# Two more pairs of gate blocks by quarter sums, and the pooling's output product moved into the attention

## The chip, the cores and the metric

The kernel runs on one core of a Trainium2 chip. The metric is the device time of one execution in microseconds (us). Before the change three runs took 1218.12, 1218.23 and 1218.29 us; the median is 1218.23.

## The reference

One layer of a streaming encoder on 1024 tokens (and 16 meta tokens ahead of them) of width 1024, all in float32:

```python
z = jnp.einsum('bld,dn->bln', u, w_in)             # u: RMS-normed input
a, q, k, v, r, lr, ga, gb = jnp.split(z, IN_SPLITS, axis=-1)   # 512, 256, 256, 512, 512, 16, 1024, 1024
p = multiscale_pool(a).reshape(B, L, POOL_GROUPS, POOL_GROUP_DIM)
p = jnp.einsum('blgc,gce->blge', p, w_pool_mix).reshape(B, L, POOL_WIDTH) * pool_scale
y_a = jnp.einsum('blc,cd->bld', p, w_pool_out)
log_a = jax.nn.log_sigmoid((lr @ w_gate_up + b_gate)) / GLA_TAU
...
o = gla_chunked(q, k, v, log_a)                    # gated linear attention, chunks of 64
o = rmsnorm(o, gla_norm) * jax.nn.silu(r)
y_b = jnp.einsum('blc,cd->bld', o, w_gla_out)
m = jax.nn.sigmoid(ga) * y_a + jax.nn.sigmoid(gb) * y_b
return jnp.einsum('bld,de->ble', m, w_out)         # then h + this, and a squared-ReLU MLP 1024-4096-1024
```

## The kernel before

**Products.** A float32 product is made of three passes (`mm3`, L250 to 257): high part by high part (L255), weights' high part by the input's low part (L256), weights' low part by high part (L257). So each operand is first split: the high part is a copy (ScalarE), the low part a subtraction (VectorE, or GpSimd in the attention). The input is kept split in `TH` and `TL`, one tile for each half of the 1024 tokens (`th`, `tl` in rows). A block is 128 columns of an output; over 1024 tokens it is 8 pieces of depth by two halves by three passes, 48 matmuls of 512 columns. Weights of a block come from HBM to a raw buffer and are split into `W1` (`w1h`, `w1l`; L83 and L87, in the attention four quarters on GpSimd).

**Stages, in the order in which TensorE runs them.** (1) Load, norm and split of the input, first values. (2) *Gate stage*: the class `Quarters` takes two blocks and both halves of the depth as a product of 2 by 2 parts, and makes it with 7 products of quarter sums in place of 8, so a pair of blocks is 7 x 12 = 84 matmuls in place of 96. `BLOCKS` lists the 16 blocks, 8 pairs: the eight of gate `ga`, two of the queries `q`, four of `r`, two of gate `gb`. Results go to HBM (`ga_dram`, `q_dram`, `r_dram`, `gb_dram`). (3) *Pooling*: four groups (`a_block`, `mean_block`, `mix_block`): the product `a`, the trailing means minus the token (`ph`, high and low), and six matmuls of the mixing. An eviction on ScalarE (L918) and one on VectorE (L919) write the pooled operand `pm` as high and low part. (4) *Pool output product*: `ya_block`, four blocks of 256 columns and 48 matmuls each, of depth 512; a unit of it (12 matmuls) is evicted by VectorE with a multiplication by the gate (L971) into `o` and stored to `ma_dram`. Group 0 is mixed inside the first block. The gates are loaded by `gate_load` into six buffers `g`. (5) *Attention*, `gla`: four units, each one pair of heads by one half of the tokens, and between their steps *filler*, so that TensorE has work while VectorE and ScalarE make scores and states: key blocks, the values' second half, six blocks of `gb` (direct, 48 matmuls each, with a sigmoid of several ScalarE and VectorE steps, L926 to 930, and an exponential), and the output product `yb`. (6) Output projection and the two MLP products, also by quarter sums.

**What sets the order.** Within a stage each engine runs its instructions in the order in which the program records them. `one` lists the steps, `fill` the filler's; `pour` takes filler by an estimate of its cost for each wait of the attention's steps. DMAs are issued by SyncE, a single queue in order; an issue that waits for a buffer holds up all behind it. Two stacks of on-chip memory, `left` and `right`, are pushed and popped at the stages' borders, so tiles of a later stage lie in the room of earlier ones, and their first writers wait for the last readers.

**Names that the steps below use.** `lr`: the 16 rows of the low-rank gate, stacked three times (`stacked`, L538 to 546: a clearing on GpSimd, two copies on ScalarE, a subtraction on VectorE), multiplied at L1170 (L1183 in the changed program) for the log-decay of a unit. `scc`: scores after the masked copy (L1290), from products at L1227. `f`, `n`: the decayed operands on VectorE (L1259, L1261). `b_...`: PSUM banks by role.

Of the kernel before, what the change touches and what calls it, by code (L numbers as in the profile page):

```python
# [15 lines left out]
P = 128  # L16
# [98 lines left out]
def kernel(  # L115
# [84 lines left out]
    def f32(ap):  # L200
        return ap.bitcast(F32)
# [49 lines left out]
    def mm3(ps, n, lhs, rhs, first=True, last=True, more=False):  # L251

        for i in range(n):
            (ah, al), (bh, bl) = lhs(i), rhs(i)
            pe.matmul(ps, ah, bh, start=first and i == 0, stop=False, skip_group_check=more)  # L255
            pe.matmul(ps, ah, bl, start=False, stop=False, skip_group_check=more)  # L256
            pe.matmul(ps, al, bh, start=False, stop=last and i == n - 1, skip_group_check=more)  # L257
# [30 lines left out]
    class Quarters:  # L288
# [61 lines left out]
        def prime(self, first=True):  # L350

            if first:
                w1 = [t.rearrange("p s (u c) -> p (s u) c", u=2) for t in (W1.hi, W1.lo)]
                S["slots"] = [(w1[0][:, i], w1[1][:, i]) for i in range(4)]
                slot_n[0] = -1
                self.rest, self.made = self.forms(), []
            self.made.append(next(self.rest))

# [189 lines left out]
    def lr_turn():  # L548
# [15 lines left out]

    BLOCKS = (
        [("ga", d, C_GA + d * P) for d in range(8)] + [("q", p, C_Q + p * P) for p in range(2)]
        + [("r", h, C_R + h * P) for h in range(HEADS)] + [("gb", d, C_GB + d * P) for d in range(2)]
    )
    gate_quarters = Quarters(
        len(BLOCKS) // 2, lambda f: w_cols(BLOCKS[f][2]), [[None, raw.own[0]], [None, raw.own[1]]],  # L570
# [288 lines left out]

    def pool_open():  # L860
        left.pop_to(left0)
        buffer("a", 2, SEQ + META)
        buffer("s", 2, SEQ + META)
        right.pop_to(0)
        S["vw"].append(right.push("vw1", [P, 2, KT, 256], F32R))
        S["pm"] = right.push("pm", [P, 2, 4, SEQ], F32R)
        S["ph"] = right.push("ph", [P, 2, SEQ], F32R)
        mw = S["mw"] = right.push("mw", [P, 2, 4, P], F32R)
        r = raw.load(w_pool_mix.rearrange("g c e -> c g e"), 4 * P).rearrange("p (g e) -> p g e", g=4)
        act.activation(mw[:, 0], r, ACT.Copy)  # L870
        pool.tensor_tensor(mw[:, 1], r, f32(mw[:, 0]), ALU.subtract)
        buffer("g", 6)
        buffer("o", 4)
        raw.lend(left.push("raw2", [P, D], F32))
        for _ in range(4):
            gate_load()

    step(one, pool_open)

# [31 lines left out]
    def mix_block(g):  # L911
        def fn():
            wb = (S["mw"][:, 0, g], S["mw"][:, 1, g])
            for tag, c in zip(("ms", "ms"), halves()):
                b = bank(tag)
                mm3(b, 1, lambda i: wb, lambda i: (S["ph"][:, 0, c], S["ph"][:, 1, c]))
                ph = S["pm"][:, 0, g, c]
                act.activation(ph, b, ACT.Copy, scale=pscale[:, g : g + 1])  # L918
                dve.scalar_tensor_tensor(S["pm"][:, 1, g, c], b, pscale[:, g : g + 1], f32(ph), ALU.mult, ALU.subtract)  # L919
                yield  # L920

        return fn
# [12 lines left out]
    def gate_load():  # L935

        n = len(gates)
        if n < 16:
            g = gates[n // 2, n % 2] = nxt("g")
            nc.sync.dma_start(g, ga_dram[n // 2, n % 2])  # L940

    def ya_block(j):
        def fn(wb):
            hi, lo = (t.rearrange("p (k c) -> p k c", k=4) for t in wb)
            pm = S["pm"]
            units = [(e, h, c) for e in range(2) for h, c in enumerate(halves())]

            def product(b, e, c, ks, first, last):
                w = slice(e * P, (e + 1) * P)
                mm3(  # L950
                    b, len(ks), lambda i: (hi[:, ks[i], w], lo[:, ks[i], w]),
                    lambda i: (pm[:, 0, ks[i], c], pm[:, 1, ks[i], c]), first=first, last=last,
                )

            early = {}
            if j == 0:
                for e, h, c in units[:3]:
                    early[e, h] = bank("mm")
                    product(early[e, h], e, c, (3, 2, 1), True, False)
                yield from mix_block(0)()  # L960
            for e, h, c in units:
                if (e, h) in early:
                    b = early[e, h]
                    product(b, e, c, (0,), False, True)
                else:
                    b = bank("mm")
                    product(b, e, c, (3, 2, 1, 0), True, True)
                if e and h:
                    yield "free"
                o = nxt("o")  # L970
                dve.tensor_tensor(o, b, gates[2 * j + e, h], ALU.mult)  # L971
                nc.sync.dma_start(ma_dram[2 * j + e, h], o)
                gate_load()
                yield 12 * 512 / 2400

        return fn

# [3 lines left out]
    a_ = lambda g: step(one, a_block(g), W1, [w_cols(C_A + g * P)])  # L981
    p_ = lambda g: step(one, mean_block(g))
    m_ = lambda g: step(one, mix_block(g))
    y_ = lambda d: step(one, ya_block(d), W1, [rows4(w_pool_out, d)])
    for f, i in (
        (a_, 3), (p_, 3), (a_, 2), (m_, 3), (p_, 2), (a_, 1), (m_, 2), (p_, 1), (a_, 0), (m_, 1), (p_, 0),
        (y_, 0), (y_, 1), (y_, 2),
    ):
        f(i)
    step(one, lambda: load_vw(1))  # L990
    y_(3)


    def gla_open():
        raw.back()
        W1.eng = pool
        right.pop_to(1)
        left.pop_to(left0)
        S["wgraw"] = right.push("wgraw", [RANK, 256], F32)
        nc.sync.dma_start(S["wgraw"], w_gate_up)  # L1000
        stacked(wgu, S["wgraw"], 2)
        S["kq"] = [left.push(f"kq{h}", [P, 2, 2, HALF + OFF[h]], F32) for h in range(2)]
        for h in range(2):
            q = S["kq"][h][:, :, 1, OFF[h] : OFF[h] + HALF]
            for p in range(2):
                nc.sync.dma_start(q[:, p], q_dram[p, h])
        S["v"].append(left.push("v1", [P, NC, 2 * P], F32))
# [6 lines left out]
        S["ends"] = left.push("ends", [P, HALF], F32)  # L1014
        S["scc"] = left.push("scc", [P, 2, 2, 4, CH], F32)
# [12 lines left out]

    def k_block(p):
        def evac(b, half, at, n):  # L1030
            act.activation(S["kq"][half][:, p, 0, at : at + n], b, ACT.Copy)

        return lambda wb: project(wb, WITH_META, evac)

    def v_second():
        for t in range(9):
            rows, leave = v_tile(1, t, by_k=True)
# [3 lines left out]
            leave()  # L1041

    def yg_open():
        right.pop_to(0)
        S["yg"] = {h: right.push(f"yg{h}", [P, 2, HEADS, HALF], F32R) for h in (1, 0)}


    def gb_block(d):
# [6 lines left out]
        return lambda wb: project(wb, MAIN, evac)  # L1055

    staged = {}

# [90 lines left out]
    def told(name):  # L1149
        step(fill, lambda: done.add(name))  # L1150

    for p in range(2):
        step(fill, k_block(p), W1, [w_cols(C_K + p * P)])
        told(("k", p))
    step(fill, v_second)
    step(fill, yg_open)
    told("v")
    for d in range(2, 8):
        step(fill, gb_block(d), W1, [w_cols(C_GB + d * P)])
    for j in range(4):  # L1160
        step(fill, yb_block(j, 0), W1, [rows4(w_gla_out, j)])

# [134 lines left out]
    def across(p, half):  # L1297
# [38 lines left out]
        for j in (3, 0, 1, 2):  # L1336
            for e, u in ((0, 0), (1, 0), (1, 1), (0, 1)):
# [2 lines left out]
                    o[part(u ^ e), e, j], qe[part(e), part(c)], states[c][part(e)], start=False, stop=True,  # L1340
                    tile_position=(e * CH, (u ^ e) * CH), skip_group_check=True,
                )
        while "v" not in done:
            yield 1.0
        sr = S["sr"].rearrange("p e t -> p (e t)")
        nc.sync.dma_start(sr.rearrange("p (e t) -> p e t", e=2), r_dram[2 * p : 2 * p + 2, half].rearrange("h p t -> p h t"))
# [27 lines left out]
    def gla():  # L1374
# [9 lines left out]
                    return  # L1384
                owed[0] -= cost

        while ("k", 0) not in done:
            next(filler)
# [444 lines left out]
```

## Time and profile before

| | |
|---|---|
| median of three runs | 1218.23 us |
| the profiled execution's own time | 1218.34 us |
| its span (first to last instruction) | 1216.1 us |
| TensorE busy | 1198.0 us, 99% |
| VectorE, ScalarE, GpSimd busy | 70%, 51%, 5% |
| gate stage | 44.6 to about 204 us |
| pooling | 201.2 to 253.2 us |
| pool output product | 253.2 to 299.3 us |
| attention with its filler | 299.3 to about 478 us |
| output projection and MLP | from 502.6 us |

Columns of the group rows are: line, engine, operation, output <- input by name, shapes, count, then busy time and the mean of one in ns, then the idle time of the engine ahead of it and what ended it. A timeline row begins with start and length in us; xN joins N equal neighbours. A wait row has the waiting instruction, what it waited for, the total, how often and the longest.

### The profile page before, as it was taken

What the parts mean: (1) busy time and instruction counts of PE and PEld (TensorE: products, weight loads), DVE (VectorE), ACT (ScalarE), POOL (GpSimd) and SP (SyncE); (2) the same over time, 40 slices, a digit from 0 to 9 for tenths busy, and PEclk for the clock granted to TensorE, in tenths of its full rate; (3) what the DMA queues carried; (4) which work ended last, traced back from release to release, by engine and by line L of the source; (5) the groups of instructions that cost most, each with busy time, mean ns of one, the idle gap of its engine ahead of it and who ended that gap; (6) DMA issues with size and microseconds to landing.
All of it is one profiled execution on the core that took longest, in us unless ns stands there. A gap on an engine that the chain in (4) does not pass through costs nothing.

```text
span 1216.1 us, 18370 instructions
## 1 busy us (share of the span) xinstructions
PE 1198.0 (99%) x6818; PEld 997.9 (82%) x6818; DVE 854.6 (70%) x1411; ACT 618.5 (51%) x1103; POOL 63.0 (5%) x100
## 2 busy tenths in 40 slices
PE   7999999999999999999999999999999999999997
PEld 7878888988887778888888888888888888888886
DVE  7996676654556677735897667676675887887686
ACT  7667567322446663324655455454554444444554
POOL 2000000001201126000000000000000000000000
PEclk9999999999999999999999999999999999999999
DMA  8043426146102246741245454344479973333532
GB/s 255 2 113 114 125 77 201 45 153 223 36 19 62 71 144 230 267 149 70 105 139 166 145 165 156 130 162 146 168 239 326 337 241 96 95 98 94 173 96 87
DMA packets 141672, 173.84 MB, mean 143 GB/s; under 512 B 9944, under 2 KB 81392, under 8 KB 141584
## 3 DMA queue, kind: packets, MB, share of 16 engines
q1 hardware_dynamic: 141552, 172.62, 44.0%
q8 instruction: 53, 0.87, 0.3%
q14 instruction: 35, 0.29, 0.1%
q0 software_dynamic: 32, 0.07, 0.1%
HBM read 119.17 MB, written 53.48 MB: 142 GB/s over the span
## 4 chain that ended last, share of the span: by engine, by line
PE 92%; DVE 4%; ACT 2%; issue 1%; DMA 0%; POOL 0%; SPq 0%; ACTq 0%; POOLq 0%; DVEq 0%
PE b_mm L255 11%; PE b_mm L256 11%; PE b_mm L257 11%; PE b_ms L257 9%; PE b_ms L255 9%; PE b_ms L256 9%; PE b_x L256 8%; PE b_x L255 8%; PE b_x L257 8%; PE b_mx L255 1%; PE b_sc L1227 1%; PE b_mx L256 1%; PE b_mx L257 1%; PE b_ms L1505 1%; DVE ut L783 1%
## 5 line engine op out<-in xcount | busy, mean ns | idle before, releaser
L255 PE MATMUL b_mm<-th,w1h 128*128 128x512 f32 (+1 forms) x312 | 117.6, 377 | 1.1 <-DVE c L818 1.0
L256 PE MATMUL b_mm<-tl,w1h 128*128 128x512 f32 (+1 forms) x312 | 115.9, 372 | 0.0
L257 PE MATMUL b_mm<-th,w1l 128*128 128x512 f32 (+1 forms) x312 | 115.9, 371 | 0.0
L255 PE MATMUL b_x<-th,w1h 128*128 128x512 f32 (+1 forms) x240 | 90.8, 378 | 0.0
L256 PE MATMUL b_x<-tl,w1h 128*128 128x512 f32 (+1 forms) x240 | 90.7, 378 | 0.0
L257 PE MATMUL b_x<-th,w1l 128*128 128x512 f32 (+1 forms) x240 | 90.3, 376 | 0.0
L273 ACT ACTIVATE w1h<-raw 128x512 fp32r<-128x512 f32 x96 | 59.5, 620 | 29.0 <-PE b_ms L256 13.7
L274 DVE TENSOR_TENSOR w1l<-raw,w1h 128x512 fp32r<-128x512 f32 x96 | 65.6, 684 | 8.6 <-ACT w1h L273 8.6
L255 PEld LDWEIGHTS b_mm<-th,w1h 128*128 128x128 f32 x312 | 58.6, 188 | 12.5 <-issue 1.9
L273 ACT ACTIVATE w1h<-fs 128x512 fp32r<-128x512 f32 x72 | 45.3, 631 | 44.9 <-PE b_ms L256 30.8
L257 PEld LDWEIGHTS b_mm<-th,w1l 128*128 128x128 f32 x312 | 58.6, 188 | 10.4
L256 PEld LDWEIGHTS b_mm<-tl,w1h 128*128 128x128 f32 x312 | 58.6, 188 | 9.8
L273 ACT ACTIVATE w1h<-bt 128x512 fp32r<-128x512 f32 x44 | 27.8, 632 | 67.1 <-issue 62.7
L274 DVE TENSOR_TENSOR w1l<-fs,w1h 128x512 fp32r<-128x512 f32 x72 | 49.2, 686 | 15.0 <-ACT w1h L273 14.9
L1681 DVE TENSOR_TENSOR bt<-w,w 128x512 f32<-128x512 f32 x80 | 54.7, 684 | 1.6 <-DMA w<-in_w_ff_dram 1.6
L257 PEld LDWEIGHTS b_x<-th,w1l 128*128 128x128 f32 x240 | 45.1, 188 | 8.5
L255 PEld LDWEIGHTS b_x<-th,w1h 128*128 128x128 f32 x240 | 45.1, 188 | 8.4
L256 PEld LDWEIGHTS b_x<-tl,w1h 128*128 128x128 f32 x240 | 45.1, 188 | 8.3
L273 ACT ACTIVATE fxh<-bt 128x512 fp32r<-128x512 f32 x36 | 22.8, 632 | 55.7 <-issue 50.1
L257 PE MATMUL b_ms<-wo,w1l 128*128 128x512 f32 x128 | 49.9, 390 | 0.0
L255 PE MATMUL b_ms<-wo,w1h 128*128 128x512 f32 x128 | 49.8, 389 | 0.0
L256 PE MATMUL b_ms<-wo,w1h 128*128 128x512 f32 x128 | 49.8, 389 | 0.0
(455 smaller groups left out, 3345.2 us busy)
## 6 DMA issues: line engine op xcount, KB each, us to landing
hf_dram<-h SPq DMA_DIRECT2D x112, 256.0 KB, 2.1
raw<-hf_dram SPq DMA_DIRECT2D x112, 256.0 KB, 2.7
w<-in_w_ff_dram SPq DMA_DIRECT2D x64, 256.0 KB, 4.8
raw<-in_w_in_dram SPq DMA_DIRECT2D x24, 512.0 KB, 4.8
raw<-in_w_ff_dram SPq DMA_DIRECT2D x16, 512.0 KB, 4.1
rawx<-in_w_ff_dram SPq DMA_DIRECT2D x16, 512.0 KB, 4.0
xs<-in_x_dram SPq DMA_DIRECT2D x8, 512.0 KB, 5.5
rawx<-in_w_in_dram SPq DMA_DIRECT2D x8, 512.0 KB, 4.4
```

Of the source, the lines that this page charges most:

```text
L255: pe.matmul(ps, ah, bh, start=first and i == 0, stop=False, skip_group_check=more)
L256: pe.matmul(ps, ah, bl, start=False, stop=False, skip_group_check=more)
L257: pe.matmul(ps, al, bh, start=False, stop=last and i == n - 1, skip_group_check=more)
L273: act.activation(hi, a, ACT.Copy)
L274: dve.tensor_tensor(lo, a, f32(hi), ALU.subtract)
L783: dve.tensor_tensor(to_, a_, b_, ALU.subtract)
L1227: pe.matmul(b[to, e, j], kk[r, s], qq[r, s], start=True, stop=True, tile_position=(e * CH, u * CH))
L1505: pe.transpose(b[j][:, i], u[:, (4 * j + i) * P : (4 * j + i + 1) * P], ident)
L1681: dve.tensor_tensor(bt, w, S["w2"][q[3:]][:, i], ALU.add if q[2] == "+" else ALU.subtract)
```

## The change

Four more gate blocks (`gb` 2 to 5) join `BLOCKS`: the gate stage has 10 pairs in place of 8, and the filler loses those four direct blocks. Since a pair has seven products and the ring of split weights four slots, the ring's start is moved so that it ends where it did (`slot_n`). The pool output product leaves the line of stages and becomes filler behind the last `gb` block. With it move: the pooled operand `pm` is kept whole, and split only during the last `gb` block's second part, into the room of the second half's input (`TH[1]`, `TL[1]`), whose product that block therefore makes first; the halves' copies are ScalarE's, the subtractions GpSimd's. The gate loads use three buffers `t1`, two loads ahead, where there were six buffers `g`. The first key block moves ahead of the attention's opening, and the last group's six mixing matmuls stand behind it. Room for keys and queries is taken at the pooling's start; the split gated output of half 0 takes the room of the second values' weights, and that of half 1 waits until `pm` is free.

```diff
-                slot_n[0] = -1
+                slot_n[0] = -1 - 7 * self.n % 4
...
-        + [("r", h, C_R + h * P) for h in range(HEADS)] + [("gb", d, C_GB + d * P) for d in range(2)]
+        + [("r", h, C_R + h * P) for h in range(HEADS)] + [("gb", d, C_GB + d * P) for d in range(6)]
...
+        S["kq"] = [left.push(f"kq{h}", [P, 2, 2, HALF + OFF[h]], F32) for h in range(2)]
+        S["left_k"] = left.mark()
...
-        S["pm"] = right.push("pm", [P, 2, 4, SEQ], F32R)
+        S["pm"] = right.push("pm", [P, 4, SEQ], F32)
...
-        buffer("g", 6)
-        buffer("o", 4)
         raw.lend(left.push("raw2", [P, D], F32))
-        for _ in range(4):
-            gate_load()
...
-                ph = S["pm"][:, 0, g, c]
-                act.activation(ph, b, ACT.Copy, scale=pscale[:, g : g + 1])
-                dve.scalar_tensor_tensor(S["pm"][:, 1, g, c], b, pscale[:, g : g + 1], f32(ph), ALU.mult, ALU.subtract)
+                act.activation(S["pm"][:, g, c], b, ACT.Copy, scale=pscale[:, g : g + 1])
...
-            g = gates[n // 2, n % 2] = nxt("g")
+            g = gates[n // 2, n % 2] = nxt("t1")
...
+            ph, pl = S["pm2"]
+            for e, (h, c) in ((e, x) for e in range(2) for x in enumerate(halves())):
+                b, w = bank("mm"), slice(e * P, (e + 1) * P)
+                for k in (3, 2, 1, 0):
+                    mm3(
+                        b, 1, lambda i: (hi[:, k, w], lo[:, k, w]), lambda i: (ph[:, k, c], pl[:, k, c]),
+                        first=k == 3, last=k == 0,
+                    )
+                    yield 3 * 512 / 2400
                 if e and h:
                     yield "free"
                 o = nxt("o")
                 dve.tensor_tensor(o, b, gates[2 * j + e, h], ALU.mult)
                 nc.sync.dma_start(ma_dram[2 * j + e, h], o)
                 gate_load()
...
-        (y_, 0), (y_, 1), (y_, 2),
...
+    step(one, queries)
+    step(one, k_block(0), W1, [w_cols(C_K)])
+    m_(0)
+    step(one, lambda: load_vw(1))
...
+    def pooled_parts():
...
+        S["pm2"] = [a[1].rearrange("p k c -> p (k c)").rearrange("p (g c) -> p g c", g=4) for a in (TH, TL)]
+        for c in halves():
+            for g in (3, 2, 1, 0):
+                (ph, pl), pm = (a[:, g, c] for a in S["pm2"]), S["pm"][:, g, c]
+                act.activation(ph, pm, ACT.Copy)
+                for q in halves_of_half:
+                    pool.tensor_tensor(pl[:, q], pm[:, q], f32(ph[:, q]), ALU.subtract)
+                yield
+
+    def gb_last(d):
+        def fn(wb):
+            parts = pooled_parts()
+            for n, cost in enumerate(gb_block(d, MAIN[::-1])(wb)):
+                if n >= KT:
+                    next(parts, None)
+                if n in (KT, KT + 1):
+                    gate_load()
+                yield cost
...
-    for d in range(2, 8):
-        step(fill, gb_block(d), W1, [w_cols(C_GB + d * P)])
+    step(fill, gb_block(6), W1, [w_cols(C_GB + 6 * P)])
+    step(fill, gb_last(7), W1, [w_cols(C_GB + 7 * P)])
+    step(fill, yg_last)
+    for j in range(4):
+        step(fill, ya_block(j), W1, [rows4(w_pool_out, j)])
...
-        while "v" not in done:
+        while ("pm" if half else "v") not in done:
```

**TensorE, where the pooling ends.** Before, the last group's mixing (`ph`, `mw`: the means and the mixing weights) stands inside the pool output product (`pm`), from the mixing on:

```order
L255 MATMUL b_ms<-ph,mw 128x512 [waits Activation_49]
L256 MATMUL b_ms<-ph,mw 128x512 [waits DVE_49]
L257 MATMUL b_ms<-ph,mw 128x512
L255 MATMUL b_mm<-pm,w1h 128x512 [waits Activation_49]
L256 MATMUL b_mm<-pm,w1h 128x512 [waits DVE_49]
L257 MATMUL b_mm<-pm,w1l 128x512
```

And the log-decay of the first unit (L1170) stood between the first key block's last matmuls and the second's, with the whole block behind the output product:

```order
L256 MATMUL b_mm<-tl_135,w1h 128x264
L257 MATMUL b_mm<-th_131,w1l 128x264 [waits DVE_49]
L1170 MATMUL b_mx<-lrT_meta,wgu 128x16 [waits DVE_49,Activation_49]
L1170 MATMUL b_ms<-lr,wgu 128x512 [waits Pool_49]
L255 MATMUL b_mm<-th_131,w1h 128x264
```

Now the key block (`th`, `tl`) comes first, then the mixing, then the log-decay (L1183):

```order
L256 MATMUL b_x<-tl_143,w1h 128x512
L257 MATMUL b_x<-th_139,w1l 128x512
L255 MATMUL b_ms<-ph,mw 128x512 [waits Activation_49]
L256 MATMUL b_ms<-ph,mw 128x512 [waits DVE_49]
L257 MATMUL b_ms<-ph,mw 128x512
L1183 MATMUL b_mm<-lrT_meta,wgu 128x16
L1183 MATMUL b_ms<-lr,wgu 128x512 [waits DVE_49,Activation_49]
L255 MATMUL b_mm<-th_131,w1h 128x264
```

The 72 matmuls of the key block stood between the mixing and the log-decay, and now stand ahead of both. `lr` lies in the room of `ph`: in the changed program its clearing on GpSimd waits for the last of those mixing matmuls.

**GpSimd, in the middle of the attention.** Before, only splits of weights stand there; after, the subtractions of the pooled operand (L1043) stand between the splits of the first (`raw_119`) and the second output block's weights (`raw_115`):

```order
L87 TENSOR_TENSOR w1l<-raw_119,w1h 128x256 [waits DMAHW3_49,Activation_49]
L87 TENSOR_TENSOR w1l<-raw_119,w1h 128x256 [waits PE_49] x3
L1043 TENSOR_TENSOR tl_143<-pm,th_139 128x256 [waits DMAHW1_49,DMAHW6_49,DMAHW0_49,Activation_49]
L1043 TENSOR_TENSOR tl_143<-pm,th_139 128x256
...
L87 TENSOR_TENSOR w1l<-raw_115,w1h 128x256 [waits DMAHW6_49,Activation_49,Pool_49]
L87 TENSOR_TENSOR w1l<-raw_115,w1h 128x256 [waits PE_49,Pool_49] x3
```

Sixteen subtractions have come between two splits.

**SyncE's queue, at the same place.** The raw load of the fourth output block's weights (L110) waits for the end of that second split on GpSimd, and behind it stand a store of `gb`, the first store of the output product (`ma_dram`, L954) and the next two gate loads (L936):

```order
L936 DMA t1_2772<-ga_dram_71 128x512 [waits DVE_49]
L1064 DMA gb_dram_72<-o_2776 128x512 [waits Activation_49]
L1359 DMA mix_2780<-r_dram_74 128x2x512 [waits DMAHW6_49,DMAHW7_49,DVE_49,PE_49]
L110 DMA raw0_115<-in_w_pool_out_dram 128x4x256 [waits Activation_49,Pool_49]
L1064 DMA gb_dram_72<-o_2776 128x512 [waits DMAHW0_49,Activation_49]
L954 DMA ma_dram_70<-o_2776 128x512 [waits DMAHW1_49,DVE_49]
L936 DMA t1_2772<-ga_dram_71 128x512 [waits DMAHW2_49]
L936 DMA t1_2772<-ga_dram_71 128x512 [waits DMAHW3_49]
```

Before, there were only raw loads, stores of `gb` and loads of `r` in this stretch; the gate loads stood in the output product's own stage.

More of the change, by code (lines that the diff above doesn't have):

```diff
@@ L944, in fn @@
             hi, lo = (t.rearrange("p (k c) -> p k c", k=4) for t in wb)
[L945 to L967, printed above, removed]
+            ph, pl = S["pm2"]
[7 more added lines that the diff above has]
+                    yield 3 * 512 / 2400
                 if e and h:
@@ L973, in fn @@
                 gate_load()
-                yield 12 * 512 / 2400
         return fn
@@ L983, with k_block, evac, queries @@
     m_ = lambda g: step(one, mix_block(g))
-    y_ = lambda d: step(one, ya_block(d), W1, [rows4(w_pool_out, d)])
     for f, i in (
         (a_, 3), (p_, 3), (a_, 2), (m_, 3), (p_, 2), (a_, 1), (m_, 2), (p_, 1), (a_, 0), (m_, 1), (p_, 0),
-        (y_, 0), (y_, 1), (y_, 2),
     ):
         f(i)
[L990 to L1002, printed above, removed]
+    def k_block(p):
+        def evac(b, half, at, n):
+            act.activation(S["kq"][half][:, p, 0, at : at + n], b, ACT.Copy)
+        return lambda wb: project(wb, WITH_META, evac)
+    def queries():
         for h in range(2):
@@ L1006, in gla_open @@
                 nc.sync.dma_start(q[:, p], q_dram[p, h])
+    step(one, queries)
+    step(one, k_block(0), W1, [w_cols(C_K)])
+    m_(0)
+    step(one, lambda: load_vw(1))
+    def gla_open():
+        raw.back()
+        W1.eng = pool
+        right.pop_to(2)
+        left.pop_to(S["left_k"])
         S["v"].append(left.push("v1", [P, NC, 2 * P], F32))
@@ L1014, in gla_open @@
         S["ends"] = left.push("ends", [P, HALF], F32)
+        wg = S["ends"][:RANK, :256]
+        nc.sync.dma_start(wg, w_gate_up)
+        stacked(wgu, wg, 2)
         S["scc"] = left.push("scc", [P, 2, 2, 4, CH], F32)
@@ L1027 @@
     step(one, gla_open)
[L1029 to L1033, printed above, removed]
     def v_second():
@@ L1043, in yg_open, with yg_last, gb_block @@
     def yg_open():
-        right.pop_to(0)
-        S["yg"] = {h: right.push(f"yg{h}", [P, 2, HEADS, HALF], F32R) for h in (1, 0)}
-    def gb_block(d):
+        S["yg"] = {0: S["vw"][1].rearrange("p n k c -> p (n k c)").rearrange("p (n h c) -> p n h c", n=2, h=HEADS)}
+    def yg_last():
+        right.pop_to(1)
+        S["yg"][1] = right.push("yg1", [P, 2, HEADS, HALF], F32R)
+        done.add("pm")
+    def pooled_parts():
[16 more added lines that the diff above has]
+                yield cost
+        return fn
+    def gb_block(d, pieces=MAIN):
         def evac(b, half, at, n):
@@ L1053, in evac @@
             nc.sync.dma_start(gb_dram[d, half], o)
-        return lambda wb: project(wb, MAIN, evac)
+        return lambda wb: project(wb, pieces, evac)
     staged = {}
@@ L1150, in told @@
         step(fill, lambda: done.add(name))
-    for p in range(2):
-        step(fill, k_block(p), W1, [w_cols(C_K + p * P)])
-        told(("k", p))
+    step(fill, k_block(1), W1, [w_cols(C_K + P)])
+    told(("k", 1))
     step(fill, v_second)
@@ L1385, in pour @@
                 owed[0] -= cost
-        while ("k", 0) not in done:
-            next(filler)
         units = [(0, 0), (1, 0), (0, 1), (1, 1)]
```

## The prediction

> **What bounds the kernel now.** I read the page first: the busy table, then the shares of the chain that ended last.
>
> ```profile
> PE 1198.0 (99%) x6818; PEld 997.9 (82%) x6818; DVE 854.6 (70%) x1411; ACT 618.5 (51%) x1103; POOL 63.0 (5%) x100
> ...
> PE 92%; DVE 4%; ACT 2%; issue 1%; DMA 0%; POOL 0%; SPq 0%; ACTq 0%; POOLq 0%; DVEq 0%
> ```
>
> TensorE is busy 99% of the span and carries 92% of the chain. So the time is about a number of matmuls times their spacing, plus the few places where TensorE waits. The busy table over four stretches says whether that holds where the change works: one pair of gate blocks (107.83 to 127.05, from a `P4` product to the next pair's), pooling, the pool output product, and the main part of the attention. Columns are the stretch, its length, then busy time (instructions) by engine, clock, DMA share and GB/s.
>
> ```profile
> 107.83:127.05 19.22, 19.22 (x85) 15.77 (x84) 13.01 (x20) 13.77 (x26) 0.00 (x0) 1.00 0.36 111
> ...
> 253.20:299.30 46.10, 45.71 (x199) 36.96 (x199) 22.05 (x27) 9.20 (x12) 4.80 (x2) 1.00 0.72 233
> ...
> 361.10:453.80 92.70, 90.74 (x1071) 72.11 (x1063) 64.70 (x128) 59.27 (x101) 15.62 (x20) 1.00 0.27 84
> ```
>
> The gate pair is TensorE alone: 19.22 of 19.22 us, VectorE (13.01) and ScalarE (13.77) with a third to spare, clock 1.00. The attention has 1.96 us of idle TensorE. What TensorE waits for there, and at the pool output product, stands in its waits over the whole run (total, times, longest):
>
> ```profile
> PE b_sc L1227 <- DVE scc L1290: 2.0, 4, 0.7
> ...
> PE b_mm L256 <- DVE pm L919: 0.3, 1, 0.3
> ```
>
> **The change, part by part.** (1) Two more pairs in the gate stage. Each costs one row of the table, 19.22 us: 2 x 19.22 = +38.44. The four blocks leave the attention's filler, but four blocks of the pool output product enter it: both are 4 x 48 matmuls of 512 columns, so the filler's amount stays: 0.
>
> (2) The pool output product's own stage goes. Its length, with the exact ends:
>
> ```profile
> 253.25:299.33 46.08, 45.69 (x199) 1.00 0.72 233
> ```
>
> It held one thing that stays, the six matmuls of the pooled mixing of group 0; the same six for another group stand just ahead of the stage, from 251.89 to 253.25, 1.36 us:
>
> ```profile
> 251.89 0.39 PE L255 MATMUL b_ms<-ph,mw 128*128 128x512 f32 x1
> ...
> 253.03 0.39 PE L257 MATMUL b_ms<-ph,mw 128*128 128x512 f32 x1
> 253.25 0.39 PE L255 MATMUL b_mm<-pm,w1h 128*128 128x512 f32 x1
> ```
>
> So -46.08 + 1.36 = -44.72. Parts 1 and 2 give 38.44 - 44.72 = **-6.28 us**. This is the 24 matmuls that the quarter sums save (12 a pair, at 19.22 / 84 = 0.229 us: 5.5 us), and some 0.8 us that the stage lost at its entry, the 0.3 on `pm` among it.
>
> A rule of the Trainium skill bears on the size: "TensorE: Matmul & The Clock Gate", Back-to-back issue gap, gives about 131 ns for each matmul of 512 columns in a stream. By it 24 matmuls would be 3.1 us and the sum of parts 1 and 2 about -3.9. The rows above have 0.229 us, for three-pass fp32, so the trace decides.
>
> (3) A wait that was covered and is no longer. The attention begins with a small chain for the log-decay: GpSimd clears `lr` (L542), ScalarE copies into it twice (L545), VectorE subtracts (L546), and only then TensorE multiplies (L1170, now L1183). Before, it ran under the 72 matmuls of the first key block:
>
> ```profile
> 299.56 0.52 POOL L542 MEMSET lr<- 80x512 f32 x1 [9.21 <-PE b_x L257]
> ```
> ```profile
> 300.27 1.26 ACT L545 ACTIVATE lr<-gB 16x512 fp32r<-16x512 f32 x2
> ```
> ```profile
> 301.66 0.68 DVE L546 TENSOR_TENSOR lr<-gB,lr 16x512 fp32r<-16x512 f32 x1
> ```
> ```profile
> 311.05 0.48 PE L1170 MATMUL b_ms<-lr,wgu 80*128 80x512 f32 x1
> ```
>
> The chain was done at 302.34 and wanted at 311.05. In the changed order the key block comes first, then the six mixing matmuls, then L1183 with nothing between. And `lr` lies in the room of `ph`, which the last mixing matmul reads, so the clearing cannot start sooner. On ScalarE the copies stand behind what follows such a mixing: the rows of the place before, at group 1.
>
> ```profile
> 251.87 1.06 ACT L83 ACTIVATE w1h<-raw 128x1024 fp32r<-128x1024 f32 x1 [3.87 <-PE b_x L256]
> 252.83 0.58 ACT L888 ACTIVATE a<-b_x 128x512 f32<-128x512 f32 x1
> 253.31 1.26 ACT L918 ACTIVATE pm<-b_ms,small 128x512 fp32r<-128x512 f32 x2
> ```
>
> Put on that clock: TensorE would be free at 253.28; ScalarE is done with both evictions at 253.31 + 1.26 = 254.57 (the clearing, 0.52 from about 253.45, is done by then); the two copies end at 255.83; the subtraction needs the first alone, 255.20 + 0.68 = 255.88. TensorE loses 255.88 - 253.28 = **+2.6 us**. Bounds: 2.2 if the records overlap by the 0.1 seen between L83 and L888, 3.3 if the subtraction waits for both copies.
>
> (4) The operand's split. Eight ScalarE copies and sixteen GpSimd subtractions of 128x256 now run in the attention, in place of eight VectorE operations (L919). The same form has two speeds in the trace, four at a time:
>
> ```profile
> 311.78 2.82 POOL L87 TENSOR_TENSOR w1l<-raw,w1h 128x256 fp32r<-128x256 f32 x4 [11.70 <-ACT w1h L83]
> 325.68 4.25 POOL L87 TENSOR_TENSOR w1l<-raw,w1h 128x256 fp32r<-128x256 f32 x4 [11.09 <-ACT w1h L83]
> ```
> ```profile
> L87 POOL TENSOR_TENSOR w1l<-raw,w1h 128x256 fp32r<-128x256 f32 x40 | 31.3, 812 | 123.1 <-ACT w1h L83 58.8 <-PE b_mx L257 39.6 <-PE b_ms L1308 13.3
> ```
>
> At the mean of 0.812 us, 16 take 13.0 us (11.3 to 17.0). GpSimd is otherwise busy 15.62 of 92.70 us, so its own time is free; the question is who stands behind. SyncE does: the raw load of the fourth output block's weights waits until GpSimd has split the second block's, which stands behind the sixteen, and the gate loads for the third and fourth unit (a unit: 12 matmuls, one eviction that multiplies by a gate) are issued after it. The units' pace: 92.70 us for 288 filler matmuls (the next rows, times three passes), 12 x 92.70 / 288 = 3.86 us.
>
> ```profile
> L255 PE MATMUL b_mm<-th,w1h 128*128 128x512 f32 x64 | 26.5, 414 | 0.0
> ...
> L255 PE MATMUL b_mx<-th,w1h 128*128 128x512 f32 x32 | 13.1, 409 | 0.0
> ```
>
> The split starts with the last half of the last gate block (24 matmuls, 7.7 us) ahead of the units, so the third gate is wanted at 7.7 + 3 x 3.86 = 19.3 us. It lands at 13.0 + 4 x 0.812 + 1.1 (raw to gate issue, 277.89 to 278.95) + 4.8 = 22.1:
>
> ```profile
> 277.89 0.38 SPq L110 DMA_DIRECT2D raw<-in_w_in_dram  x1
> ...
> 278.95 0.42 SPq L940 DMA_DIRECT2D g<-ga_dram  x1
> ```
> ```profile
> DMA to landing us min/median/max: 2.9/4.8/5.8
> ```
>
> VectorE thus waits about 2.8 us once; TensorE feels what is queued behind on VectorE and not hidden by two further PSUM banks. I take a quarter, **+0.7**, bounds 0 and 2.8. The other raw loads among the gate loads stand behind a split that takes 2.8 to 4.3 us after a block's end, and the next unit's product is evicted 3.86 + 0.7 us after it: 0.
>
> (5) VectorE and ScalarE in the attention. VectorE's waits there:
>
> ```profile
> DVE t L930 <- ACT t L929: 13.2, 7, 3.0
> ```
>
> The sigmoids and this wait go; sixteen multiplications of 0.69 us come for eight subtractions of the sigmoids. I take the 2.0 us of TensorE's waits on `scc` as they are: 0, bounds -2.0 (all gone) and +3 (each of them over twice as long).
>
> **Sum**: -6.28 + 2.6 + 0.7 = -3.0 us on the profiled execution's 1218.34 (span 1216.1 and 2.2 around it). The median shown is 1218.23, so **1215.2**. Bounds together: -6.28 + 2.2 + 0 - 2.0 = -6.1 and -6.28 + 3.3 + 2.8 + 3 = +2.8.
>
> **Rivals.** A: the attention gains. VectorE loses a wait of 13.2 us, so the masked copies come sooner, and the 2.0 us of TensorE's waits go. For it: those waits and VectorE's stand in the same stretch. Against: the multiplications now wait for a DMA instead. It gives 1215.2 - 2.0 = 1213.2.
>
> B: the attention loses somewhat. The splitting makes VectorE or GpSimd slower where both work, the parts come late for the first unit, and `scc` is later. For it: two speeds of one GpSimd form, 0.70 and 1.06. Against: VectorE's own operations in that stretch stay at one mean, whatever GpSimd does.
>
> ```profile
> L1261 DVE TENSOR_TENSOR f<-n,ends 128x512 f32<-128x512 f32 x10 | 6.8, 684 | 0.0
> L1259 DVE TENSOR_TENSOR n<-n,ends 128x512 f32<-128x512 f32 x10 | 6.8, 683 | 0.0
> ```
>
> It gives 1215.2 + 1 to + 5, middle 1218. The Trainium skill has the rule for it: "SBUF — State Buffer", Who interferes with whom and the section on the two sides, describes a port pair that VectorE and GpSimd hold exclusively for a whole instruction, when VectorE reads two operands from SBUF. By it sixteen subtractions could hold VectorE up to 11 us; the rows here show the loss on GpSimd's side, and none on VectorE's.
>
> C, the slower one: the gate loads do not keep up. The loads run two units ahead in three buffers, and each is queued on SyncE behind the store of the unit before. A gate is there 0.69 (multiplication) + 0.9 (two issues) + its landing after a unit's end, and wanted 2 x 3.86 = 7.7 us after it. It decides from a landing of 6.1 us; the median in the trace is 4.8 and the longest 5.8, at a DMA share of 0.72, and the attention's share is 0.27, which speaks against it. At a landing of 6.6 us each of 14 units is 0.5 us late on VectorE, with nothing hidden: +7, **1222**.
>
> D: the change does not save what it says, because a gate pair more is not 19.22 us, as VectorE or stores limit the stage. With 13.01 of 19.22 us busy this needs a third more of VectorE's work; at 20.5 us a pair it would give 1217.8, and it is counted with B.
>
> **How the numbers follow.** The forecast, 1213.9 to 1217, has 0.50; A 0.14; B and D 0.24; C 0.12. Within 0.2% (about what a measurement of this kernel can tell from no change) is 1215.8 to 1220.7. Of the forecast's 0.50 some 0.06 lies above 1215.8, so faster is 0.44 + 0.14 = 0.58; within 0.06 + 0.22 = 0.28, as 0.02 of B passes the bound; slower 0.12 + 0.02 = 0.14. The range of 8 in 10 goes from the lower bound, 1212.1, to 1220: A and nearly all of B are in it, C is left out.
>
> **What would show it.** The gate stage longer by 38.4 us, its spacing unchanged. A stretch of idle TensorE of some 2.6 us before L1183, released by VectorE or ScalarE on `lr`. One VectorE wait of 2 to 3 us at L953 on a gate load and none later. TensorE's waits on `scc` at 2 us in all. The forecast is wrong if a gate pair takes over 19.4 us, if the chain of `lr` shows no wait, or if VectorE waits for many gates.

## The result, and the profile after

The changed kernel takes 1220.21 us (median of 20 runs, 1217.61 to 1221.81) against 1218.14 (20 runs, 1217.74 to 1218.99): a ratio of 1.0016, interval 1.0010 to 1.0022. It is slower by 2.1 us, where 3.0 us less were forecast. Its runs also spread over 4.2 us, where the 20 before spread over 1.25, and the profiled execution, 1217.61, is the fastest of the twenty. So two things ask for an explanation: why even the fastest is not at 1215, and why most are slower than it.

Most of the change did what it says. The gate stage, in the busy table of the changed kernel (a pair from `P4` to `P4`, the pair behind it, and the whole stage):

```profile
126.86:146.08 19.22, 19.22 (x85) 15.77 (x84) 12.42 (x19) 12.26 (x23) 0.00 (x0) 1.00 0.38 110
146.08:165.31 19.23, 19.23 (x86) 15.78 (x84) 11.68 (x18) 8.99 (x16) 0.00 (x0) 1.00 0.36 109
44.47:239.40 194.93, 193.90 (x863) 158.38 (x862) 143.91 (x214) 134.06 (x232) 0.00 (x0) 1.00 0.35 106
```

A pair is 19.22 us as before, so rival D is out. The page's busy table and chain have TensorE at 98% and 85%:

```profile
PE 1191.6 (98%) x6794; PEld 993.0 (82%) x6794; DVE 869.7 (72%) x1432; ACT 626.3 (52%) x1123; POOL 75.0 (6%) x112
...
PE 85%; DVE 8%; ACT 3%; DMA 2%; issue 1%; SPq 0%; POOL 0%; DVEq 0%; POOLq 0%; ACTq 0%
```

TensorE's busy time is 6.4 us less, close to the 6.3 of the sum, and of the seven points that it lost in the chain four have gone to VectorE. What VectorE held up stands in TensorE's waits from 290 to 480 us:

```profile
PE b_m L1342 <- DVE S L1335: 3.5, 1, 3.5
PE b_ms L1183 <- DVE lr L546: 2.5, 1, 2.5
PE b_sc L1240 <- DVE scc L1303: 0.7, 1, 0.7
PE b_m L1342 <- DVE W L1335: 0.5, 1, 0.5
...
```

Before, the same stretch had one row, 2.0 us on `scc`; that is 0.7 now, with 1.1 us of small waits that are new (on `W`, which is made on the same line as the states `S`, and on two tiles left out of the rows). The wait on `lr` is the one forecast: in the timeline L1183's two matmuls start at 304.20 and 306.86, 2.66 us apart, against 2.6.

```profile
304.20 0.17 PE L1183 MATMUL b_mm<-lrT_meta,wgu 80*128 80x16 f32 x1
306.86 0.47 PE L1183 MATMUL b_ms<-lr,wgu 80*128 80x512 f32 x1 [2.49 <-DVE lr L546]
```

The wait of 3.5 us ahead of L1342 (scores by values, which needs the states `S` that VectorE makes at L1335) was forecast by no term. In VectorE's groups from 382.8 to 391 us, just ahead of it, operations are longer than most of their form; the three small ones take over three times what they take from 391 us on (224, 192 and 176 ns). Four of the rows:

```profile
L1274 DVE TENSOR_TENSOR f<-n,mix 128x512 f32<-128x512 f32 x1 | 1.2, 1231 | 0.0
...
L1276 DVE TENSOR_TENSOR ends<-ends 128x64 f32<-128x64 f32 x1 | 0.8, 759 | 0.0
...
L1276 DVE TENSOR_TENSOR ends<-ends 128x16 f32<-128x16 f32 x1 | 0.6, 647 | 0.0
L1276 DVE TENSOR_TENSOR ends<-ends 128x32 f32<-128x32 f32 x1 | 0.6, 633 | 0.0
```

and GpSimd's timeline shows what ran beside them: ten of the sixteen subtractions of the pooled operand.

```profile
376.01 4.67 POOL L1043 TENSOR_TENSOR tl<-pm,th 128x256 fp32r<-128x256 f32 x6
382.87 8.13 POOL L1043 TENSOR_TENSOR tl<-pm,th 128x256 fp32r<-128x256 f32 x10 [2.19 <-ACT th L1041]
```

For the spread, each run's mean granted clock (the share of TensorE's full clock that it was given, averaged over the span) is the first hint. Of the twenty, two have 0.998 and eighteen 0.997 to 0.994; the lowest clocks, 0.994, go with 1221.3 to 1221.8.

Two theories follow. **Theory 1**: the two idle stretches cost their length, and beyond it they make the chip lower TensorE's clock for some us in most executions. **Theory 2**: the spread has another source, such as the transfers, which the change rearranged. Beside these, the wait ahead of L1342 had two explanations: GpSimd's subtractions hold VectorE up, or there is simply more in the queues.

### The profile page after: what moved, and what is told of

Same layout as the page of the kernel before. It is cut to its first block, busy times and chain, and to the rows that moved or that the text cites. A ratio compares the mean times of both kernels' runs of the same rounds, so it can differ in the third digit from the quotient of the medians.

```text
span 1215.8 us, 18356 instructions
## 1 busy us (share of the span) xinstructions
PE 1191.6 (98%) x6794; PEld 993.0 (82%) x6794; DVE 869.7 (72%) x1432; ACT 626.3 (52%) x1123; POOL 75.0 (6%) x112
## 4 chain that ended last, share of the span: by engine, by line
PE 85%; DVE 8%; ACT 3%; DMA 2%; issue 1%; SPq 0%; POOL 0%; DVEq 0%; POOLq 0%; ACTq 0%
PE b_mm L255 10%; PE b_mm L257 9%; PE b_mm L256 9%; PE b_ms L256 9%; PE b_ms L255 9%; PE b_ms L257 9%; PE b_x L256 8%; PE b_x L255 8%; PE b_x L257 8%; PE b_sc L1240 1%; PE b_mx L255 1%; PE b_mx L257 1%; PE b_mx L256 1%; DVE w1l L274 1%; DVE ut L783 1%
## 5 line engine op out<-in xcount | busy, mean ns | idle before, releaser
L255 PE MATMUL b_x<-th,w1h 128*128 128x512 f32 (+1 forms) x264 | 100.2, 380 | 0.0
L256 PE MATMUL b_x<-tl,w1h 128*128 128x512 f32 (+1 forms) x264 | 100.1, 379 | 0.0
L257 PE MATMUL b_x<-th,w1l 128*128 128x512 f32 (+1 forms) x264 | 99.7, 378 | 0.0
L273 ACT ACTIVATE w1h<-fs 128x512 fp32r<-128x512 f32 x78 | 49.0, 630 | 48.4 <-PE b_ms L256 34.1
L274 DVE TENSOR_TENSOR w1l<-fs,w1h 128x512 fp32r<-128x512 f32 x78 | 53.4, 686 | 16.3 <-ACT w1h L273 16.2
L257 PEld LDWEIGHTS b_x<-th,w1l 128*128 128x128 f32 x264 | 49.7, 188 | 9.5
L255 PEld LDWEIGHTS b_x<-th,w1h 128*128 128x128 f32 x264 | 49.5, 188 | 9.5
L256 PEld LDWEIGHTS b_x<-tl,w1h 128*128 128x128 f32 x264 | 49.6, 188 | 9.3
L273 ACT ACTIVATE w1h<-rawx 128x512 fp32r<-128x512 f32 x44 | 27.5, 629 | 44.2 <-PE b_x L256 18.6
L255 PE MATMUL b_ms<-wo,w1h 128*128 128x512 f32 x128 | 49.8, 389 | 0.0
```

Of the source, the lines that this page charges most:

```text
L273: act.activation(hi, a, ACT.Copy)
L274: dve.tensor_tensor(lo, a, f32(hi), ALU.subtract)
```

## The experiments

Line numbers in the rows shift by a few lines from kernel to kernel; L1183 and L1342 name the places in the changed kernel throughout the text.

**The changed kernel as it is**, with the clock of each of 11 executions.

> The changed kernel as it is, for the spread of its executions and the granted clock of each. Theory 1: TensorE's new idle stretches (2.7 us ahead of L1183, 3.9 us ahead of L1342) lower the granted clock for some us in many executions; then single times spread over 1217.5 to 1222 and each 0.001 of mean clock is worth about 1.2 us. Theory 2: the spread comes from the transfers; then times and clock have no fixed relation.

1220.0 us, 1217.28 to 1221.44. Two executions have 0.998 or 0.999 and 1217.3 to 1217.5; the other nine 0.997 to 0.994 and 1219.1 to 1221.4. Of 33 runs of the kernel before on the same chip none is below 0.998. Time and clock are tied, as theory 1 wants.

**`lr` out of the room of `ph`.**

```diff
         S["left_n"] = left.mark()
+        S["lr"] = left.push("lr", [P, HALF], F32R)
         S["N"] = [left.push(f"n{i}", [P, HALF, 2], F32) for i in range(2)]
...
-        S["lr"] = left.push("lr", [P, HALF], F32R)
```

> lr lies below the other tiles, out of the room of ph, so its chain runs before the pooling and L1183 has nothing to wait for. Sum of the waits: the fastest executions at 1217.6 - 2.6 = 1215.0. Theory 1, if the stretch ahead of L1183 lowers the clock: every execution at 0.997 or more and a median near 1215.5; if the one ahead of L1342 does: the spread stays at 4 us and the median is about 1217.6. Theory 2: median 1217.6 with the same spread.

1218.24 us (1216.54 to 1219.56). The chain on `lr` runs before the pooling now, but half of the wait stays: L1183 now waits 1.2 us for the PSUM bank that the mixing's eviction (L915) has to free. The median falls by 1.8 us, and nine of 11 are still below 0.998. The trace is of an execution at 0.997, and shows where. Columns: stretch, length, TensorE busy, granted clock, DMA share, GB/s.

```profile
380.00:387.00 7.00, 7.00 (x88) 1.00 0.24 64
387.00:391.60 4.60, 1.32 (x6) 1.00 0.21 80
391.60:395.00 3.40, 3.23 (x67) 0.67 0.13 36
395.00:400.00 5.00, 5.00 (x77) 0.89 0.83 296
```

The clock is full through the idle stretch ahead of L1342 and lower behind it: (0.33 x 3.4 + 0.11 x 5) / 0.5 = 3.3 us at half clock. Such a stretch of lower clock is called a dip below.

**The low parts on VectorE.** `dve.tensor_tensor(pl, pm, f32(ph), ALU.subtract)` in place of the loop of GpSimd's halves.

> The sixteen subtractions of 128x256 that make the pooled operand's low part are eight of 128x512 on VectorE in place of GpSimd. If VectorE is held up by GpSimd's subtractions (its small operations were 0.43 to 0.54 us longer beside them, 2.8 us in all), the wait ahead of L1342 shrinks from 3.9 to under 1.5 us and the fastest executions are at 1214 to 1216. If only VectorE's order of work makes that wait, 8 x 0.69 = 5.5 us more on VectorE lengthen it to 5 us or more, 1219 and up. Theory 1: with the wait under 1.5 us the spread shrinks if that stretch lowers the clock.

1219.06 us (1216.83 to 1220.56). The wait does not shrink: 3.3 us on `S`, 0.5 on `W`. Five of the eight subtractions, 0.7 us each and one 1.0, stand in VectorE's queue in the same stretch. The expectation took the one theory or the other; the work costs VectorE about the same whether it does it or is held up by it.

**Both edits.**

> Both edits: lr out of ph's room and the low parts on VectorE. If the two waits are all that is lost against the sum of the matmuls, about 1212 to 1213.5, at a clock of 0.998 in every execution by theory 1; by theory 2 the same fastest time with a spread of 4 us.

1217.57 us (1216.86 to 1218.16), nine of 11 below 0.998. The forecast of 1212 to 1213.5 fell with the wait that parts_dve kept.

**Without the split** (`next(parts)` makes nothing).

```diff
-                act.activation(ph, pm, ACT.Copy)
-                for q in halves_of_half:
-                    pool.tensor_tensor(pl[:, q], pm[:, q], f32(ph[:, q]), ALU.subtract)
                 yield
```

> The changed kernel without the split of the pooled operand: neither the eight copies nor the sixteen subtractions are made, so the pool output product multiplies what is left of the input there. Theory 1: the split's work on ScalarE, GpSimd and VectorE makes the wait of 3.9 us ahead of L1342, so that wait falls under 1 us, the fastest executions to about 1214, and the clock is lower only by the stretch of 2.7 us ahead of L1183: 0.997 or more. Rival: the wait comes from the order of the filler, which is the same here; then it stays over 3 us.

1215.12 us (1213.78 to 1216.36): the wait on `S` is gone, only 0.5 on `W` is left, so the filler's order does not make it. Four of 10 executions are below 0.998; with the stretch ahead of L1183 alone, the clock still falls in some.

**Without the subtractions only**, the eight copies kept.

> The changed kernel with the eight copies of the pooled operand but without the sixteen GpSimd subtractions, so the operand's low part is not made. If GpSimd's hold on VectorE makes most of the wait ahead of L1342 (2.8 us of VectorE's operations were longer beside it), the wait is about 1 us; if the copies on ScalarE, which stand between the steps of the log-decay, make it, it stays at 2.5 us or more.

1216.53 us (1214.29 to 1217.82). TensorE's waits, 290 to 480 us:

```profile
PE b_ms L1181 <- DVE lr L546: 2.5, 1, 2.5
PE b_m L1340 <- DVE S L1333: 0.7, 1, 0.7
...
PE b_m L1340 <- DVE W L1333: 0.5, 1, 0.5
```

So GpSimd's subtractions make 2.8 of the 3.5 us, and ScalarE's copies 0.7. VectorE's groups in this kernel, from 376 to 392 us, answer to those shown above:

```profile
L1272 DVE TENSOR_TENSOR f<-n,mix 128x512 f32<-128x512 f32 x1 | 0.7, 685 | 0.0
...
L1274 DVE TENSOR_TENSOR ends<-ends 128x64 f32<-128x64 f32 x1 | 0.2, 219 | 0.0
L1274 DVE TENSOR_TENSOR ends<-ends 128x32 f32<-128x32 f32 x1 | 0.2, 191 | 0.0
L1274 DVE TENSOR_TENSOR ends<-ends 128x16 f32<-128x16 f32 x1 | 0.2, 174 | 0.0
```

0.647 us beside GpSimd, 0.174 without, for 16 columns: the loss is 0.44 to 0.55 us in these four operations, whatever their size, and 0.42 in the one ahead of them (128 columns, 0.707 for 0.292). It isn't so for every operation there: in the same stretch one of 256 columns took 0.427 for 0.421, and those that read `b_m` in PSUM 0.343 for 0.340.

**No wait ahead of L1183**: `lr` as above, and the mixing of group 0 inside the first key block.

```diff
-    step(one, k_block(0), W1, [w_cols(C_K)])
-    m_(0)
+    def k_and_mix(wb):
+        for n, cost in enumerate(k_block(0)(wb)):
+            yield cost
+            if n == 15:
+                yield from mix_block(0)()
...
+    step(one, k_and_mix, W1, [w_cols(C_K)])
```

> lr out of ph's room, and the six mixing matmuls of group 0 moved between the second and the third piece of the first key block, so that L1183 has neither lr nor its PSUM bank to wait for. Waits: 2.7 us less than the changed kernel, 1.3 less than the first of these edits alone; fastest executions at 1214.7. Theory 1: the clock as in the first edit (one dip of 3.4 us at half clock, 0.997), median about 1217; if the stretch ahead of L1183 had no part in the clock, the median falls by just 2.7 to 1217.4 and the spread stays at 4 us.

1216.86 us (1215.1 to 1218.1), eight of 11 below 0.998; the wait ahead of L1183 is gone from the trace. The fastest is 2.2 to 2.5 us faster than the changed kernel's, the median 2.9 to 3.4 (against its three sets of runs).

**Neither wait**: this, and no split.

> Both removed: lr_free's edits, and the split of the pooled operand left out. By the sum of the matmuls (two pairs more, the output product's stage gone: -6.3 us, and 1.3 us of waits on scc that are gone) about 1211, at a clock of 0.998 or more in every execution and a spread like that of the kernel before, 2 us. If the lower clock comes from something else than idle TensorE, the spread stays at 4 us.

1211.55 us (1211.12 to 1212.23), 0.998 or more in all five, a spread of 1.1 us. TensorE's waits from 290 to 480 us:

```profile
PE b_sc L1242 <- DVE scc L1305: 0.7, 1, 0.7
PE b_m L1344 <- DVE W L1337: 0.5, 1, 0.5
PE b_m L1372 <- DVE mix L1368: 0.4, 1, 0.4
...
```

This is the change without its two idle stretches (and without the split's work): 6.6 us less than before. The wide spread has gone with them, though all the transfers of the change are still there, which is against theory 2.

**A longer stretch ahead of L1183**, without the split again: four clearings of `lr` more ahead of the chain.

> The changed kernel without the split of the pooled operand (it leaves that out), and with four clearings of lr more ahead of its first copies, so that the only long idle stretch of TensorE, ahead of L1183, is about 4.1 us instead of 2.7. Theory 1: with a longer stretch every execution has a dip of the clock, 0.997 or less in all, and the median is more than the 1.4 us later: 1215.1 + 1.4 + about 1 = 1217.5. If idle time does not set the clock, half of the executions stay at 0.998 and the median is at 1216.5.

1218.28 us (1217.62 to 1218.96). The wait is 4.7 us, 2.2 more than in no_parts; the median is 3.2 later, so 1.0 is not the wait's length. Nine of 11 are below 0.998 where no_parts had four of 10, and five are at 0.995. Theory 1 expected a dip in all. The two at 0.998 don't decide that: they took 1217.64 and 1217.95 us, as long as the traced execution (1217.7, at 0.996), whose trace has one dip.

**The split drawn out**: the second half's parts behind the last gate block, in the first half's input tile.

> lr_free's edits, and the pooled operand's split drawn out: the first half's parts as before during the last gate block's second piece but one for every two steps, the second half's only behind that block, in the first half's freed input tile, while the first output block makes its two units of the first half of the tokens. GpSimd's subtractions then stand beside VectorE's chain of states by half as many. By the theory that GpSimd's hold on VectorE makes the wait ahead of L1342, it falls from 3.9 to about 1.5 us, and the time from 1216.9 to about 1214 at a clock of 0.998 or more in nearly every execution. If the number of instructions in the queues makes it, the wait stays over 3 us and the time at 1216.9.

1216.66 us, the wait at 3.5. It tells nothing on the reason, since the edit did not move the work: the tile's first slices come free while the block still runs, and the subtractions stand where they stood.

```profile
380.91 8.13 POOL L1055 TENSOR_TENSOR tl<-pm,th 128x256 fp32r<-128x256 f32 x10 [2.18 <-ACT th L1053]
```

**The split sooner**: no wait ahead of L1183, and both last gate blocks make their second half of the tokens first, so the input's room is free 24 matmuls sooner. Both blocks' weights are held for as long.

```diff
+        for n, (d, half) in enumerate(((0, 1), (1, 1), (0, 0), (1, 0))):
...
+            for i, cost in enumerate(project(wbs[d], [MAIN[half]], evac, free=n == 3)):
+                if n >= 2:
+                    next(parts, None)
```

> lr_free's edits, and both last gate blocks make their second half of the tokens first, so that the split of the pooled operand begins 24 matmuls (about 7.7 us) sooner and is done before VectorE's chain of states ahead of L1342. All instructions stay. If GpSimd's hold on VectorE in that stretch makes the wait, it falls from 3.9 to under 1.5 us, and the median from 1216.9 to about 1213, at 0.998 or more in nearly every execution. If the number of instructions makes the wait, 1216.9 as before.

1213.74 us (1213.17 to 1214.15, five runs), a ratio to the kernel before of 0.9962, interval 0.9948 to 0.9976: faster than both kernels, with the whole computation. All five are at 0.998 or more. GpSimd is done with the sixteen at 376.5, ahead of the chain that begins at 377.7; what stays is 1.9 us. The split of the next weights now stands beside the chain; whether it makes the rest was not tested.

```profile
363.99 12.47 POOL L1052 TENSOR_TENSOR tl<-pm,th 128x256 fp32r<-128x256 f32 x16 [30.73 <-ACT th L1050]
377.18 4.33 POOL L87 TENSOR_TENSOR w1l<-raw,w1h 128x256 fp32r<-128x256 f32 x4 [0.72 <-ACT w1h L83]
```
```profile
PE b_m L1347 <- DVE S L1340: 1.9, 1, 1.9
```

**The changed kernel again, three times, for a trace of a lowered clock.**

> The changed kernel once more, for a trace of an execution at a mean clock below 0.998. Theory 1: one or more stretches of 3.4 us at half clock, each starting within some us behind the wait ahead of L1183 or the one ahead of L1342, and nowhere else in the program.

1219.74 us (1217.61 to 1221.7, eight runs, clocks 0.998 to 0.994); the traced one was at 0.998 and has no dip.

> The changed kernel, for a trace at a mean clock below 0.998. Theory 1: stretches of 3.4 us at half clock, each within some us behind the wait ahead of L1183 or ahead of L1342 and nowhere else.

1220.29 us at 0.995, and the trace has two dips:

```profile
303.00:307.00 4.00, 1.60 (x8) 1.00 0.12 13
307.00:311.00 4.00, 3.92 (x23) 0.71 0.41 120
311.00:315.00 4.00, 4.00 (x30) 0.86 0.02 6
315.00:320.00 5.00, 5.00 (x83) 1.00 0.00 0
320.00:384.00 64.00, 63.94 (x850) 1.00 0.13 43
384.00:389.20 5.20, 5.20 (x80) 1.00 0.27 56
389.20:393.00 3.80, 1.78 (x8) 1.00 0.34 130
393.00:397.00 4.00, 2.56 (x64) 0.63 0.02 5
397.00:401.00 4.00, 4.00 (x85) 0.94 0.99 326
401.00:406.00 5.00, 5.00 (x34) 1.00 0.36 116
406.00:500.00 94.00, 92.17 (x866) 1.00 0.64 211
500.00:1216.00 716.00, 709.87 (x3159) 1.00 0.48 159
```

At each of the two waits, from near its end on, the clock is at half for some 3.4 us ((0.29 x 4 + 0.14 x 4) / 0.5 = 3.4; (0.37 x 4 + 0.06 x 4) / 0.5 = 3.4), and full everywhere else from 303 us to the last matmul. In finer stretches it is 0.50 from 308.70 to 312.10 and from 394.00 to 397.40. The first matmul of L1183 starts at 304.42 and the last one ahead of L1342's wait at 390.60; without a dip they start at 304.20 and 388.87.

```profile
304.42 0.17 PE L1183 MATMUL b_mm<-lrT_meta,wgu 80*128 80x16 f32 x1
...
307.08 0.47 PE L1183 MATMUL b_ms<-lr,wgu 80*128 80x512 f32 x1 [2.49 <-DVE lr L546]
```
```profile
390.60 0.39 PE L257 MATMUL b_mm<-th,w1l 128*128 128x512 f32 x1
394.44 0.49 PE L1342 MATMUL b_m<-v,scc 64*64 64x128 f32 x4 [3.45 <-DVE S L1335]
```

That is 86.18 us for 84.67: the first dip costs 1.5 us. Of the 2.7 us by which this span (1218.5) is longer, about 1.0 is left for the second. An execution at 0.994, the lowest, was not traced.

> The same once more, with the same expectation: at a mean clock of 0.996 one or two such stretches, at 0.998 none.

1217.98 us at 0.998, no dip.

**All sixteen traces together.** Nine have no dip, with a mean clock of 0.9976 to 0.9990; six have one, with 0.9963 to 0.9975; `look_2` has two. The mean is below 1 even without a dip because the clock is at half in the last 2.4 to 5.8 us too, behind the last matmul, where it costs TensorE nothing. So below 0.998 there was a dip, but a rounded 0.998 can hide one, as in the trace of `no_subs`. Between two changes of the clock lie whole multiples of 3.413 us in every trace (24 of them, 81.92 us, between the two dips of `look_2`). On this grid, the 3.413 us ahead of each of the eight dips hold 1.8 to 3.3 us of idle TensorE, and no dip follows less than 1.8; between 1.8 and 1.9 both occur. The grid starts at another place in each execution, so the same wait falls on it differently from run to run.

## Why the prediction was wrong

**Parts 1 and 2, the matmuls: right.** -6.28 us were forecast; with both waits gone the change measures 1211.55 - 1218.14 = -6.6. The spans of the two traces, 1216.1 and 1209.8, differ by 6.3; the rest lies outside the span (2.2 us before, 1.8 after). The waits on `scc` are 1.3 us less in it, but four small new ones between 290 and 480 us make the same sum.

**Part 3, the wait ahead of L1183: right in place and size**, 2.66 us for 2.6, with the chain as it was worked out. What failed is that the wait was priced at its length alone.

**Part 4, the operand's split: the step that failed first.** It followed the sixteen subtractions to SyncE's queue and a late gate, for 0.7 us. No gate was late: VectorE never waited for one. The split's price was on VectorE itself, in the chain of states ahead of L1342, 3.5 us with the copies' share. The prediction had this as rival B and gave it less weight with the words that the rows show the loss "on GpSimd's side, and none on VectorE's". It read means of ten over a stretch in which GpSimd was busy for a sixth of the time. Single rows of the kernel before, next to the 4.25 us group at 325.68 that the prediction itself quoted, have it:

```profile
326.89 1.22 DVE L1261 TENSOR_TENSOR f<-n,ends 128x512 f32<-128x512 f32 x1
...
329.26 1.22 DVE L1261 TENSOR_TENSOR f<-n,ends 128x512 f32<-128x512 f32 x1
...
331.92 0.69 DVE L1261 TENSOR_TENSOR f<-n,ends 128x512 f32<-128x512 f32 x1
```

1.22 us beside GpSimd and 0.69 after it (of the two `n` beside it, one took 0.87 and one 0.67 as usual). The rule of the Trainium skill that stood there ("SBUF — State Buffer", the section on the two sides: a port pair that one of the two engines holds for a whole instruction while the other waits) was the better guide: the runs agree with it, since an operation of 16 columns loses nearly as much (0.47 us) as one of 512 (0.55).

**What no step had: the clock.** The sum with the waits as they turned out, 1211.55 + 2.66 + 3.5 = 1217.7, is the changed kernel's time at full clock (1217.3 to 1218.0 in the executions at 0.998 or more, with one exception at 1220.08). The median is 2.5 us above it, and this is the dips. No mean clock is below 0.998 in 95 runs of the kernel before on these chips nor in the ten of neither and early_pool, in which the longest wait is 1.9 us; and of every kernel with a wait of 2.5 us or more, four of 10 (no_parts) to 18 of 20 executions (the changed kernel) are below it. The Trainium skill, "TensorE: Matmul & The Clock Gate", Part 1, says that the array's clock falls to half after an idle window of about 3.4 us, and that the window runs free, so that it varies from run to run. The traces agree with the half and with the run-to-run part, and with 3.4 us as a dip's length; but an idle stretch of 2.5 us is enough in some executions (the traces of no_parts and no_subs have a dip behind one). The price is 1.0 to 1.5 us for a dip in look_2, on top of the wait.

**Part 5**: the waits on `scc` fell by 1.3 us of the 2.0 that rival A had, and small new ones of 1.1 us took most of that back. **Rival C** did not happen. Both the range and the sign fell with part 4 and the clock: 3.5 us where 0.7 were reckoned, and about 2.5 us of clock where nothing was; -6.6 + 2.7 + 3.5 + 2.5 = +2.1.

## What to carry to other kernels

Where TensorE has been busy without a break, price a new idle stretch of more than some 2 us at its length and one or two us more, since the clock may fall near its end; and look at the spread of the runs and each run's clock before explaining a median. When work moves to GpSimd, look for single rows of VectorE beside GpSimd's instructions, not for means, and place it where VectorE waits for something else: here that move made the difference between 1216.86 and 1213.74. A tile's place in memory is part of the order of work: `lr` in the room of `ph` put a whole chain behind the last matmul.

## What was not expected of the hardware

A dip takes 3.4 us at half clock, mostly when TensorE is at work again: in look_2 the first begins 1.6 us behind the end of its wait (308.7 for 307.08), the second 0.4 us ahead of it (394.03 for 394.44). And VectorE's loss beside GpSimd goes by the instruction and not by its size, 0.42 to 0.55 us in five of them beside subtractions of 0.81 us, so a chain of four operations that takes 1.3 us alone took 3.3.
